# Second feed-forward of a hybrid decoder block: tile pairs three and four moved into the seven-product form

## The chip, the core and the metric

One core of a Trainium2 chip runs the whole block in one program. The metric is the device time of that program in microseconds (us): 994.03 us is the median of three runs before the change. The engines named below are TensorE (PE, its matmuls; PEld, its weight loads), VectorE (DVE), ScalarE (ACT), GpSimd (POOL) and the queue that issues the loads (SP).

## The reference, cut to what matters

The block is a feed-forward, a token mixer, a second feed-forward and a final norm, for one sequence of 512 tokens and D_MODEL = 1024, all in float32. The change is in the second feed-forward; D_FF is 2816, which makes 22 tiles of 128 in each half of `w_in`.

```
def swiglu(u, w_in, w_out):
    a, b = jnp.split(u @ w_in, 2, axis=-1)
    return (jax.nn.silu(a) * b) @ w_out
...
        u = modulate(rmsnorm(h, g_norm_ffn2[l]), sh3, sc3)
        h = h + 0.5 * gt3 * swiglu(u, w_ffn2_in[l], w_ffn2_out[l])
    return rmsnorm(h, g_final)
```

## The kernel before, in words

**Number format.** Every float32 operand x is held as two tiles, a rounded high part (ACT copies it, L319 for weights) and a low part x - high (DVE subtracts, L333 for weights). A product is three matmuls: high by high, high by low, low by high (`mm3`, L364 to L366). The activations u of the norm stand in UH and UL: 8 slices (k) of 512 tokens, whose halves the code calls A (tokens 0 to 255) and Bh.

**Weights.** SP loads 128x1024 pieces into three `raw` buffers (and, in the feed-forwards, into parts of the tile X that have come free). `split_hi` makes the high part in a ring `whi`, `split_lo` the low part in a ring `wlo`; the rings hold seven such pieces and 128 columns over. A piece that would run over the ring's end is written in two parts, 896 and 128 columns. `take` hands out the next piece; `look(n)` splits up to n pieces ahead. For some pieces (`self.outer`) the low part is not made by DVE: ACT writes minus the high part to `wlo` (L315) and a POOL DMA adds the weight to it (L317).

**Plain pairs.** Tile pair j is the 128 columns j of the a half and of the b half. In the plain form a pair takes 48 matmuls with 512 tokens each (`ffn_tile`, twice).

**Seven products.** `duo(j)` does pairs j and j+1 together: the 2x2 block product in seven block products instead of eight, with sums of blocks on both sides. Product i is `product(...)`, 24 matmuls of 256 tokens (L755 to L757). The seven pieces of weights, in order, are r11, x0 = r12 - r11, x1 = r22 - x0, r21, r12 (replaced by r22 - r12), r22, x0 = r21 - x1; DVE makes the differences (`make`, L258). On the side of u, the blocks of sums S0, S1, S2 (`SH`/`SL`) and S3 (put over the first half of u in the second token half) come from `u_steps` once per feed-forward: sums on DVE (L714), high parts on ACT (L719), low parts on DVE (L722). The products use u itself, S0, S1, u, S2, S3, u. Product 0 goes to PSUM bank A, which ACT copies to bank C before product 2 adds to A (`copy(C, A)`, L762); after product 4 ACT copies A to a tile `u3`, before product 6 adds to A.

**Order of work.** Nothing is reordered by a scheduler: each engine runs its instructions in the order in which the code issues them, and waits in place. Before the change the second feed-forward (n = 2) runs like this: `head` computes pairs 0 and 1 in two token halves (four tiles of weights taken at once, 96 matmuls for each half) while the norm is still producing u (L472 scales to `ut`, L484 writes UH, L489 a plain copy of u for the sums, L498 UL), with three splits in between (`split(self.done)`); in the middle PE needs the row statistics of the second half (ACT square root L457, DVE reciprocal L460, PE spread L465). `ffn2` then runs seven of `u_steps`, `ffn_post` for pairs 0 and 1 (silu on ACT L685, product on DVE L658, split L667/L668), the plain pairs 2 and 3, `duo(4)`, and goes on with `out_quad` (the output matrix, in the same seven-product form) and further `duo`s.

Of the kernel before, what the change touches and what calls it, by code (L numbers as in the profile page):

```python
# [124 lines left out]

PLAIN = {0: 8, 2: 4}
PARTS = ((0, 4), (4, 8), (8, 12), (12, 16), (16, 20), (20, 22))
# [15 lines left out]
class Kernel:  # L143
# [6 lines left out]
    def plan(self):  # L150
# [21 lines left out]
        def blocks(recs, outer=0, rest=()):  # L172
            n = len(self.loads)
            if outer:
                self.outer.update({len(self.order) + 3: n + 3, len(self.order) + 5: n + 2})
            if outer == 3:
                self.outer[len(self.order)] = n
# [18 lines left out]
        def ffn(n, ins, outs, first):  # L196
# [4 lines left out]
            for part, (k0, k1) in enumerate(PARTS):  # L201
                while j < pairs_before(n, part):
                    if j < PLAIN[n]:
                        plain(ins[at:at + 2])
                        if n and j < 2:
                            shift(2)
                        j, at = j + 1, at + 2
                    else:
                        blocks(ins[at:at + 4], 2 if j > PLAIN[n] else 0)
                        j, at = j + 2, at + 4  # L210
# [270 lines left out]
    def norm_u(self, n, k, hs, t, rest=True):  # L481
# [3 lines left out]
        if n == 0 and rest:  # L485
            self.norm_x(k, hs, t)
        if n == 2 and (hs.start or k < 4):
            u = self.U4[1][k // 4] if hs.start else self.cs
            act(u[:, k % 4 * HT:(k % 4 + 1) * HT], t[:, hs], AF.Identity, bias=S, scale=1.0)  # L489
# [34 lines left out]
    def out_tail(self, ms, ksrc, gate, nxt, squares):  # L524
# [7 lines left out]
        for h, hs in enumerate((A, Bh)):  # L532
            for m in ms:
# [20 lines left out]
                if h == 1:  # L554
                    self.held = starts[m + 1]
                    if step:
                        step(1 if m != ms[-1] else 3)
                self.split_lo()
# [58 lines left out]
    def head(self, n, banks, table):  # L617
# [7 lines left out]
        both, late = list(range(4)), (0, 1, 2)  # L625
        steps = [(k, late) for k in range(4)] + [(k, (3,)) for k in range(4)] + [(k, both) for k in range(4, KT)]
        for h, hs in enumerate((A, Bh)):
            for i, (k, which) in enumerate(steps if h == 0 else [(k, both) for k in range(KT)]):
# [11 lines left out]
                if h == 0 and i < 4:  # L640
                    for x, y in ((0, 0), (1, 0), (0, 1)):
                        for j in which:
                            self.nc.tensor.matmul(banks[j][:, hs], w[j][k][x], (self.UH, self.UL)[y][k][:, hs],
                                                  start=k == x == y == 0, stop=False)
                    continue
                for j in which:
                    self.mm3(banks[j][:, hs], *w[j][k], self.UH[k][:, hs], self.UL[k][:, hs], k == 0, k == KT - 1)
                if (h, i) in ((0, 8), (1, 2), (1, 5)):
# [59 lines left out]
    def u_steps(self, n):  # L708
# [17 lines left out]

        def whole(u, k):
            x = slice(k, k + 4)
            hi, lo = (y.rearrange("p (k t) -> p k t", k=KT)[:, x, :HT] for y in (self.UHv, self.ULv))
            return lambda: v.tensor_tensor(u.rearrange("p (k t) -> p k t", k=4), hi, lo, op=OP.add)  # L730

        return ([whole(a12, 4)] if n else []) + [
            add(a22, a21, a22, OP.add), both(high(0, a22), add(a21, a11, a21, OP.subtract)),
            both(high(2, a21), low(0, a22)), add(a11, a22, a11, OP.subtract), both(high(1, a11), low(2, a21)),
            add(a12, a12, a11, OP.subtract), low(1, a11)], both(high(3, a12), low(3, a12))

# [22 lines left out]
    def duo(self, j, first):  # L759
# [64 lines left out]
    def h_sums(self, k0, first):  # L824
# [17 lines left out]
        for n, what in enumerate(((lambda: add(h22, h21, h22, OP.add),),  # L842
# [4 lines left out]
            for f in what:  # L847
                self.later((2 if k0 + 4 > first else 4) + n, f)

# [202 lines left out]
    def ffn2(self):  # L1052
# [24 lines left out]
    def open_ffn(self, nh):  # L1077
# [8 lines left out]
        self.Xall = xp.tile([P, 4 * D], F32, name="X")  # L1086
        a11, a21, a12, a22 = (self.Xall[:, i * D:(i + 1) * D] for i in range(4))
        if nh == 6:
            self.kept, a11 = [self.cond, self.AR, a11], self.cs
        self.U4, self.X, self.rawx = ((a11, a12), (a21, a22)), [a11, a21], [a12, a22]  # L1090
        return st
# [13 lines left out]
    def ffn(self, n, j, last=None):  # L1105
# [12 lines left out]
        for part, (k0, k1) in enumerate(PARTS[:-1]):  # L1118
            while j < pairs_before(n, part):
# [3 lines left out]
                else:  # L1123
                    if j == k1:
                        self.h_sums(k0, PLAIN[n])
                    self.duo(j, last)
# [702 lines left out]
```

## Time and profile before

| what | value |
|---|---|
| median of three runs | 994.03 us (993.3 to 995.08) |
| the profiled execution: its own time | 995.64 us |
| its span, first to last instruction | 993.8 us |
| granted TensorE clock, mean | 0.994 |
| second feed-forward: first matmul of `head` | 655.89 us |
| ... first plain pair after `head` | 680.06 us |
| ... first matmul of the first `duo` | 701.85 us |

Rows of the timeline read: start, duration, engine, line, operation, output<-inputs, shape, count, and in brackets how long the engine stood idle before and what ended that. Where two instructions of an engine follow each other without idle time, the difference of their starts is what the first costs. Rows of the windows give, for a stretch, the busy time of each engine, then the granted clock and the share of the DMA engines.

### The profile page before, as it was taken

The page shows a single profiled execution, that of the slowest core. Times are in us where ns is not written, and L with a number is a line of the kernel's source. Part 1 is how long each engine was busy: PE and PEld are TensorE (multiplying, and loading weights), DVE is VectorE, ACT ScalarE, POOL GpSimd, SP SyncE. Part 2 cuts the span into 40 slices and gives each one's busy share as a digit, 9 for nine tenths or more (in the row PEclk, how much of TensorE's full clock was granted, in tenths as well). Part 3 has the DMA queues.
Part 4 walks back from the last instruction along what each step waited for, and adds up shares of the span by engine and source line. Part 5 has one row for each costly group of instructions (what it writes and reads, how often), then busy time and mean ns, then how long its engine had stood idle before and what let it go on. Part 6 is the DMA issues. An engine that isn't in the chain of part 4 may idle for free.

```text
span 993.8 us, 17278 instructions
## 1 busy us (share of the span) xinstructions
PE 981.3 (99%) x6962; PEld 916.8 (92%) x6962; DVE 825.9 (83%) x1258; ACT 567.2 (57%) x869; POOL 72.4 (7%) x82
## 2 busy tenths in 40 slices
PE   8999999999999999999999999999999999999997
PEld 6888899999999999889978888898999999999996
DVE  6979989999998777879567777578898989989875
ACT  6453276786778753233414323455676768677665
POOL 0000010110111000007100000000010010011001
PEclk9999999999999999999999999999999999999998
DMA  9867577877858723123365774333376566667622
GB/s 337 281 206 261 181 185 206 222 185 215 241 145 191 212 70 93 55 94 112 105 231 170 276 247 136 102 88 104 112 181 178 148 170 161 179 141 199 168 46 85
DMA packets 50034, 166.97 MB, mean 168 GB/s; under 512 B 5665, under 2 KB 8993, under 8 KB 49954
## 3 DMA queue, kind: packets, MB, share of 16 engines
q1 hardware_dynamic: 41778, 137.95, 40.5%
q0 software_dynamic: 7488, 27.27, 16.4%
q8 instruction: 54, 0.88, 0.4%
q10 hardware_dynamic: 688, 0.66, 0.2%
q14 instruction: 26, 0.21, 0.1%
HBM read 163.08 MB, written 2.77 MB: 167 GB/s over the span
## 4 chain that ended last, share of the span: by engine, by line
PE 92%; DVE 6%; issue 1%; ACT 1%; DMA 1%; SPq 0%; DVEq 0%; ACTq 0%
PE bank L364 10%; PE bank L756 10%; PE bank L366 10%; PE bank L365 10%; PE bank L755 10%; PE bank L757 10%; PE bank L877 6%; PE bank L876 6%; PE bank L878 6%; PE bank L1759 1%; PE bank L1763 1%; PE bank L1761 1%; PE bank L1350 1%; DVE wlo L333 1%; DVE qz L1275 1%
## 5 line engine op out<-in xcount | busy, mean ns | idle before, releaser
L333 DVE TENSOR_TENSOR wlo<-raw,whi 128x1024 fp32r<-128x1024 f32 (+6 forms) x124 | 135.6, 1103 | 44.5 <-ACT whi L319 44.3
L319 ACT ACTIVATE whi<-raw 128x1024 fp32r<-128x1024 f32 (+5 forms) x157 | 149.3, 963 | 10.7 <-DMA raw<-wf1o 4.9
L364 PE MATMUL bank<-UH,whi 128*128 128x512 f32 (+1 forms) x408 | 151.6, 372 | 0.0
L366 PE MATMUL bank<-UH,wlo 128*128 128x512 f32 (+1 forms) x408 | 147.5, 362 | 0.0
L365 PE MATMUL bank<-UL,whi 128*128 128x512 f32 (+1 forms) x408 | 147.3, 361 | 0.0
L755 PE MATMUL bank<-UH,whi 128*128 128x256 f32 x512 | 141.4, 276 | 0.0
L757 PE MATMUL bank<-UH,wlo 128*128 128x256 f32 x512 | 141.4, 276 | 0.0
L756 PE MATMUL bank<-UL,whi 128*128 128x256 f32 x512 | 141.4, 276 | 0.0
L755 PE MATMUL bank<-SH,whi 128*128 128x256 f32 x384 | 107.0, 279 | 0.0
L757 PE MATMUL bank<-SH,wlo 128*128 128x256 f32 x384 | 106.9, 278 | 0.0
L756 PE MATMUL bank<-SL,whi 128*128 128x256 f32 x384 | 106.8, 278 | 0.0
L319 ACT ACTIVATE whi<-X 128x1024 fp32r<-128x1024 f32 (+2 forms) x98 | 92.0, 953 | 14.8 <-DVE X L258 14.7
L756 PEld LDWEIGHTS bank<-UL,whi 128*128 128x128 f32 x512 | 96.2, 188 | 0.1
L755 PEld LDWEIGHTS bank<-UH,whi 128*128 128x128 f32 x512 | 96.1, 188 | 0.1
L757 PEld LDWEIGHTS bank<-UH,wlo 128*128 128x128 f32 x512 | 96.1, 188 | 0.0
L333 DVE TENSOR_TENSOR wlo<-X,whi 128x1024 fp32r<-128x1024 f32 (+2 forms) x79 | 82.3, 1057 | 12.5 <-ACT whi L319 12.4
L366 PEld LDWEIGHTS bank<-UH,wlo 128*128 128x128 f32 x408 | 76.8, 188 | 12.1
L365 PEld LDWEIGHTS bank<-UL,whi 128*128 128x128 f32 x408 | 76.7, 188 | 11.4 <-issue 0.5
L364 PEld LDWEIGHTS bank<-UH,whi 128*128 128x128 f32 x408 | 76.7, 188 | 11.3 <-issue 0.5
L876 PE MATMUL bank<-HI,whi 128*128 128x256 f32 x288 | 79.9, 277 | 0.0
L877 PE MATMUL bank<-HK,whi 128*128 128x256 f32 x288 | 79.5, 276 | 0.0
L878 PE MATMUL bank<-HI,wlo 128*128 128x256 f32 x288 | 79.5, 276 | 0.0
(355 smaller groups left out, 2481.6 us busy)
## 6 DMA issues: line engine op xcount, KB each, us to landing
ada<-wada SPq DMA_DIRECT2D x47, 512.0 KB, 5.4
raw<-wmix SPq DMA_DIRECT2D x44, 512.0 KB, 4.1
raw<-wf1i SPq DMA_DIRECT2D x33, 512.0 KB, 6.3
raw<-wf2i SPq DMA_DIRECT2D x31, 512.0 KB, 4.6
AR<-wada SPq DMA_DIRECT2D x16, 512.0 KB, 3.7
wlo<-wf2i POOLq DMA_DIRECT2D x16, 512.0 KB, 5.9
raw<-wf1o SPq DMA_DIRECT2D x15, 512.0 KB, 5.2
X<-wf2i SPq DMA_DIRECT2D x13, 512.0 KB, 7.3
```

What stands on the lines that cost most here:

```text
L319: self.nc.scalar.activation(self.hi[:, y], r[:, x], AF.Copy)
L333: self.nc.vector.tensor_tensor(self.lo[:, y], r[:, x], self.hi[:, y], op=OP.subtract)
L364: M(ps, hi, uh, start=start, stop=False)
L365: M(ps, hi, ul, start=False, stop=False)
L366: M(ps, lo, uh, start=False, stop=stop)
L755: M(o, hi, uh, start=start and p == 0 and k == 0, stop=False, skip_group_check=True)
L756: M(o, hi, ul, start=False, stop=False, skip_group_check=True)
L757: M(o, lo, uh, start=False, stop=k == 3, skip_group_check=True)
L876: M(o, hi, uh, start=start and m % 2 == 0 and k == 0, stop=False, skip_group_check=True)
L877: M(o, hi, ul, start=False, stop=False, skip_group_check=True)
L878: M(o, lo, uh, start=False, stop=k == 1, skip_group_check=True)
L1275: self.nc.vector.tensor_scalar(qz[:, (2 * i + h) * P:(2 * i + h + 1) * P], q[:, toks], self.hmask[:, h:h + 1], None, op0=OP.mult)
```

## The change

`PLAIN[2]` goes from 4 to 2: pairs 2 and 3 of the second feed-forward become a `duo(2)` ahead of `duo(4)`, straight behind `head`. What that needs is moved with it:

- the two plain pieces that `head` split ahead, and the next one, are now r11, x0 and x1 of `duo(2)`; r11's low part goes by ACT and POOL DMA (`outer` = 1), and in `duo(4)` two low parts do (`outer` = 2; it had none);
- `norm_u` also writes the plain copy of u for k = 4 to 7 of half A (four more ACT instructions), and the DVE sum that made it from UH and UL (`whole`) goes;
- the sums of u are done in another order: S0, S1, S2, then the sum for S3, with five steps between `head` and `ffn_post`; they stand in other parts of X and in `cs`, the weight differences in `cond` and X, the results `kept` in X, `AR` and `cs`;
- `head` does one norm step fewer in the tail of the mixer before the last sum of squares, and a bank's halves start as one group;
- `duo(2)` looks three to five pieces ahead, not five; PSUM banks are dealt out in another order.

```
-PLAIN = {0: 8, 2: 4}
+PLAIN = {0: 8, 2: 2}
...
-            if outer:
+            if outer > 1:
                 self.outer.update({len(self.order) + 3: n + 3, len(self.order) + 5: n + 2})
-            if outer == 3:
+            if outer in (1, 3):
                 self.outer[len(self.order)] = n
...
-                        blocks(ins[at:at + 4], 2 if j > PLAIN[n] else 0)
+                        blocks(ins[at:at + 4], 2 if j > PLAIN[n] else n // 2)
...
-        if n == 2 and (hs.start or k < 4):
-            u = self.U4[1][k // 4] if hs.start else self.cs
+        if n == 2:
+            u = self.cs if k < 4 and not hs.start else self.U4[1 if hs.start else 0][k // 4]
...
-                        step(1 if m != ms[-1] else 3)
+                        step(1 if m != ms[-1] else 3 if nxt == 1 else 2)
...
-        return ([whole(a12, 4)] if n else []) + [
-            add(a22, a21, a22, OP.add), both(high(0, a22), add(a21, a11, a21, OP.subtract)),
-            both(high(2, a21), low(0, a22)), add(a11, a22, a11, OP.subtract), both(high(1, a11), low(2, a21)),
-            add(a12, a12, a11, OP.subtract), low(1, a11)], both(high(3, a12), low(3, a12))
+        last = both(high(3, a12), low(3, a12))
+        if n:
+            return [add(a22, a21, a22, OP.add), both(high(0, a22), add(a21, a11, a21, OP.subtract)), low(0, a22),
+                    add(a11, a22, a11, OP.subtract), high(1, a11), low(1, a11), high(2, a21), low(2, a21),
+                    add(a12, a12, a11, OP.subtract)], last
...
-            self.look(5)
+            self.look(3 + i // 3 if first and self.nh == 6 else 5)
...
-        self.banks, self.bi = [*f, *bk[:2], f[0], *bk[2:], f[1], *f[2:], *bk[:2], *f[:2]], 0
+        self.banks, self.bi = [*f[:2], bk[0], *f[2:], bk[1], *bk[2:], bk[0], f[2], *f[:2]], 0
...
-        do(3)
+        do(5)
         for j in range(2):
             self.ffn_post(j, self.ffn_silu(j, bk[2 * j]), bk[2 * j + 1], lambda low: (do(1), low()))
-        pa = self.ffn_tile()
         do(len(self.todo))
         self.free.append(self.rawx[1])
-        due = []
-        self.ffn_post(2, self.ffn_silu(2, pa), self.ffn_tile(), due.append)
-        pa = self.ffn_tile(4)
-        due.pop()()
-        self.ffn_post(3, self.ffn_silu(3, pa), self.ffn_tile(5), lambda low: self.later(1, low))
-        self.ffn(2, 4, last)
+        self.ffn(2, 2, last)
...
+            self.U4, self.X, self.rawx = ((self.cs, a12), (a21, a22)), [self.cond, a11], [a12, a21]
+            self.kept = [a22, self.AR, self.cs]
```

How instructions move is shown at three places. The line numbers of the change's file are a few higher (L720 for L714, L725 for L719, L728 for L722, L664 for L658, L673/L674 for L667/L668, L691 for L685, L767 for L762).

In the order rows a number behind a name tells buffers of one name apart. Rows of the two kernels stand apart.

**First place: DVE at the end of `head`'s second token half.** Before, from the low part for k = 5 to the first sums of u (`ut` is the scaled norm, `UL` its low part, `wlo` the low part of a piece of weights, `cs` and X hold blocks of u):

```order
L498 SCALAR_TENSOR_TENSOR UL<-ut,mod,UH 128x256
L333 TENSOR_TENSOR wlo<-raw_67,whi 128x1024
L472 SCALAR_TENSOR_TENSOR ut<-H_79,mod,bank_97 128x256
L498 SCALAR_TENSOR_TENSOR UL<-ut,mod,UH 128x256 x2
L730 TENSOR_TENSOR X<-UH,UL 128x1024
L714 TENSOR_TENSOR X<-X 128x1024
L714 TENSOR_TENSOR X<-cs,X 128x1024
```

The same place in the changed kernel:

```order
L498 SCALAR_TENSOR_TENSOR UL<-ut,mod,UH 128x256
L258 TENSOR_TENSOR X<-raw_68,cond 128x1024
L333 TENSOR_TENSOR wlo<-cond,whi 128x1024
L472 SCALAR_TENSOR_TENSOR ut<-H_79,mod,bank_97 128x256
L498 SCALAR_TENSOR_TENSOR UL<-ut,mod,UH 128x256 x2
L333 TENSOR_TENSOR wlo<-X,whi 128x1024
L720 TENSOR_TENSOR X<-X 128x1024
L720 TENSOR_TENSOR X<-cs,X 128x1024
```

The low part ahead of the last scaling is now that of x0 (which stands in `cond`), the weight difference x1 and the low part of x1 stand ahead of the first sum of u, and `whole` (L730) is gone.

**Second place: DVE behind the first two sums of u.** Before, from the product for pair 0 on (`sl` and `u` are silu results, `HI`/`HK` the split results of a pair):

```order
L658 TENSOR_TENSOR cond<-sl,bank_102 128x512
L722 TENSOR_TENSOR SL_6044<-X,SH_6043 128x1024
L668 TENSOR_TENSOR HK<-cond,HI 128x256
L658 TENSOR_TENSOR cond<-u_6322,bank_100 128x512
L714 TENSOR_TENSOR cs<-X,cs 128x1024
L668 TENSOR_TENSOR HK<-cond,HI 128x256
L333 TENSOR_TENSOR wlo<-raw_68,whi 128x1024
```

The same place in the changed kernel, down to the low part of the fourth piece of weights, r21:

```order
L728 TENSOR_TENSOR SL_6040<-X,SH_6039 128x1024
L720 TENSOR_TENSOR cs<-X,cs 128x1024
L664 TENSOR_TENSOR X<-sl,bank_102 128x512
L728 TENSOR_TENSOR SL_6043<-cs,SH_6042 128x1024
L674 TENSOR_TENSOR HK<-X,HI 128x256
L664 TENSOR_TENSOR X<-u_6331,bank_100 128x512
L674 TENSOR_TENSOR HK<-X,HI 128x256
L728 TENSOR_TENSOR SL_6045<-X,SH_6044 128x1024
L720 TENSOR_TENSOR X<-X,cs 128x1024
L258 TENSOR_TENSOR raw_67<-raw_68,raw_67 128x1024
L333 TENSOR_TENSOR wlo<-raw_66,whi 128x896
L333 TENSOR_TENSOR wlo<-raw_66,whi 128x128
```

A low part of S0 and the third sum now stand ahead of the product for pair 0, and r12' = r22 - r12 ahead of the low part of r21, which is now the piece in two parts.

**Third place: ACT from the end of `head` to the first copy of bank A.** Before, the rows behind `head`, then, behind the plain pairs, the rows in the first `duo` up to its copy (L762):

```order
L719 ACTIVATE SH_6043<-X 128x1024
L685 ACTIVATE sl<-bank_98 128x512
L667 ACTIVATE HI<-cond 128x256
L719 ACTIVATE SH_6048<-X 128x1024
L685 ACTIVATE u_6322<-bank_103 128x512
L667 ACTIVATE HI<-cond 128x256
L319 ACTIVATE whi<-raw_68 128x1024
...
L667 ACTIVATE HI<-AR 128x512
L319 ACTIVATE whi<-raw_66 128x1024
L762 ACTIVATE bank_99<-bank_98 128x512
```

In the changed kernel the first `duo` follows `head` at once (the first row is the high part of x1):

```order
L319 ACTIVATE whi<-X 128x1024
L725 ACTIVATE SH_6039<-X 128x1024
L725 ACTIVATE SH_6042<-cs 128x1024
L691 ACTIVATE sl<-bank_98 128x512
L673 ACTIVATE HI<-X 128x256
L691 ACTIVATE u_6331<-bank_103 128x512
L673 ACTIVATE HI<-X 128x256
L725 ACTIVATE SH_6044<-X 128x1024
L319 ACTIVATE whi<-raw_66 128x896
L319 ACTIVATE whi<-raw_66 128x128
L767 ACTIVATE bank_98<-bank_99 128x512
```

All three high parts of sums, both pairs' silu and split, and the two parts of r21's high part now stand between `head` and the copy of bank A.

More of the change, by code (lines that the diff above doesn't have):

```diff
@@ L626, in head, with put @@
         steps = [(k, late) for k in range(4)] + [(k, (3,)) for k in range(4)] + [(k, both) for k in range(4, KT)]
+        M = self.nc.tensor.matmul
+        def put(j, k, x, y):
+            M(banks[j][:, hs], w[j][k][x], (self.UH, self.UL)[y][k][:, hs], start=h == k == x == y == 0,
+              stop=k == KT - 1 and x == 1, skip_group_check=True)
         for h, hs in enumerate((A, Bh)):
@@ L642, in head @@
                         for j in which:
-                            self.nc.tensor.matmul(banks[j][:, hs], w[j][k][x], (self.UH, self.UL)[y][k][:, hs],
-                                                  start=k == x == y == 0, stop=False)
+                            put(j, k, x, y)
                     continue
                 for j in which:
-                    self.mm3(banks[j][:, hs], *w[j][k], self.UH[k][:, hs], self.UL[k][:, hs], k == 0, k == KT - 1)
+                    for x, y in ((0, 0), (0, 1), (1, 0)):
+                        put(j, k, x, y)
                 if (h, i) in ((0, 8), (1, 2), (1, 5)):
@@ L725, in both @@
             return lambda: [f() for f in fs]
[L727 to L730, printed above, removed]
-        return ([whole(a12, 4)] if n else []) + [
-            add(a22, a21, a22, OP.add), both(high(0, a22), add(a21, a11, a21, OP.subtract)),
-            both(high(2, a21), low(0, a22)), add(a11, a22, a11, OP.subtract), both(high(1, a11), low(2, a21)),
-            add(a12, a12, a11, OP.subtract), low(1, a11)], both(high(3, a12), low(3, a12))
+        last = both(high(3, a12), low(3, a12))
[3 more added lines that the diff above has]
+                    add(a12, a12, a11, OP.subtract)], last
+        return [add(a22, a21, a22, OP.add), both(high(0, a22), add(a21, a11, a21, OP.subtract)),
+                both(high(2, a21), low(0, a22)), add(a11, a22, a11, OP.subtract), both(high(1, a11), low(2, a21)),
+                add(a12, a12, a11, OP.subtract), low(1, a11)], last
     def step(self):
@@ L847, in h_sums @@
             for f in what:
-                self.later((2 if k0 + 4 > first else 4) + n, f)
+                self.later((2 if k0 > first else 4) + n, f)
     def out_quad(self, k0, gate, tail=None):
@@ L1087, in open_ffn @@
         a11, a21, a12, a22 = (self.Xall[:, i * D:(i + 1) * D] for i in range(4))
+        self.U4, self.X, self.rawx = ((a11, a12), (a21, a22)), [a11, a21], [a12, a22]
         if nh == 6:
-            self.kept, a11 = [self.cond, self.AR, a11], self.cs
-        self.U4, self.X, self.rawx = ((a11, a12), (a21, a22)), [a11, a21], [a12, a22]
+            self.U4, self.X, self.rawx = ((self.cs, a12), (a21, a22)), [self.cond, a11], [a12, a21]
+            self.kept = [a22, self.AR, self.cs]
         return st
@@ L1124, in ffn @@
                     if j == k1:
-                        self.h_sums(k0, PLAIN[n])
+                        self.h_sums(k0, 0 if n else 4)
                     self.duo(j, last)
```

## The prediction

> **What bounds the kernel now.** First the page: how busy each engine is, and of what the chain that ended last consists.
>
> ```profile
> PE 981.3 (99%) x6962; PEld 916.8 (92%) x6962; DVE 825.9 (83%) x1258; ACT 567.2 (57%) x869; POOL 72.4 (7%) x82
> ...
> PE 92%; DVE 6%; issue 1%; ACT 1%; DMA 1%; SPq 0%; DVEq 0%; ACTq 0%
> ```
>
> PE bounds the program. Any edit counts by the matmul time that it removes and the waits that it brings to PE. Next the windows of the stretches that change: the plain pairs, the first `duo`, a later `duo` (us of window; PE, PEld, DVE, ACT, POOL busy; clock).
>
> ```profile
> 680.06:701.85 21.79, 21.79 (x99) 18.02 (x98) 20.43 (x22) 11.79 (x16) 0.00 (x0) 1.00 0.30 97
> 701.85:721.17 19.32, 19.32 (x169) 19.32 (x168) 16.78 (x20) 14.10 (x19) 0.93 (x1) 1.00 0.50 144
> 740.21:759.41 19.20, 19.20 (x170) 19.20 (x169) 16.34 (x22) 9.82 (x14) 1.29 (x2) 1.00 0.64 168
> ```
>
> PE is full in all three, at clock 1.00. But behind `head` DVE is nearly full too (20.43 of 21.79): the plain pairs are when DVE catches up on the sums of u. The timeline of PE gives the borders and the only wait of this feed-forward before its last stage, 0.48 for the norm.
>
> ```profile
> 662.55 0.71 PE L465 MATMUL bank<-cst,r 128*128 128x128 f32 x4 [0.48 <-DVE r L460]
> ...
> 680.06 0.39 PE L364 MATMUL bank<-UH,whi 128*128 128x512 f32 x1
> ...
> 701.85 0.28 PE L755 MATMUL bank<-UH,whi 128*128 128x256 f32 x1
> 704.67 0.28 PE L755 MATMUL bank<-SH,whi 128*128 128x256 f32 x1
> 707.55 0.28 PE L755 MATMUL bank<-SH,whi 128*128 128x256 f32 x1
> 710.29 0.28 PE L755 MATMUL bank<-UH,whi 128*128 128x256 f32 x1
> ```
>
> Products 0, 1 and 2 of the first `duo` take 2.82, 2.88 and 2.74; the rest, (721.17 - 710.29) / 4 = 2.72 each.
>
> **Matmuls, -2.59.** Gone: 21.79 + 19.32 = 41.11. In their place a first `duo` at 19.32 and a steady one at 19.20, 38.52. Eight products of work become seven, but 96 matmuls of 512 take 21.79 and 168 of 256 take 19.3, so the step is worth 12%, and 2.59 us. That the first `duo` keeps its pace beside `head`'s debris is the assumption; pitches of 2.72 against 2.88 bound it at 10 x 0.14 = 1.4 either way, and I take 0.
>
> The Trainium skill ("TensorE: Matmul & The Clock Gate", section "Back-to-back issue gap") states a sustained 131 ns per matmul of 512 and 81 ns per one of 128. By it the plain pairs would take 96 x 0.131 = 12.6 us, and 168 matmuls of a width between would take 13.6 us or more, so this change would lose time on PE itself. The trace's 21.79 / 96 = 227 ns speaks against it, and the sum doesn't use it.
>
> **Four more ACT copies in half A, +0.17.** ACT at the end of half A with DVE's reciprocal, and what a copy costs (starts 0.40 apart):
>
> ```profile
> 655.69 0.50 ACT L489 ACTIVATE cs<-ut,mod 128x256 f32<-128x256 f32 x1
> 656.09 0.49 ACT L484 ACTIVATE UH<-ut,mod 128x256 fp32r<-128x256 f32 x1
> ...
> 659.82 0.51 ACT L484 ACTIVATE UH<-ut,mod 128x256 fp32r<-128x256 f32 x1 [0.52 <-DVE ut L472]
> 660.61 0.51 ACT L484 ACTIVATE UH<-ut,mod 128x256 fp32r<-128x256 f32 x1 [0.28 <-DVE ut L472]
> 661.39 0.51 ACT L484 ACTIVATE UH<-ut,mod 128x256 fp32r<-128x256 f32 x1 [0.28 <-DVE ut L472]
> 661.81 0.24 ACT L457 ACTIVATE r<-bank,eps 128x2 f32<-128x2 f32 x1
> 662.34 0.16 DVE L460 RECIPROCAL r<-r 128x2 f32<-128x2 f32 x1
> ...
> 663.81 0.51 ACT L484 ACTIVATE UH<-ut,mod 128x256 fp32r<-128x256 f32 x1 [0.46 <-DVE ut L472]
> ```
>
> Most of four copies (1.6) fits into waits of 0.52, 0.28 and 0.28. The square root moves from 661.81 to 662.23 and ends at 662.47; the reciprocal, which stood at 662.34 behind DVE's last UL, goes to 662.51. PE's spread moves from 662.55 to 662.72, and so does all behind it. If the copies hid wholly it is 0, with none hidden 1.6; I take 0.17.
>
> **Three splits in half B, and when u's sums can start.** In half B ACT now has work where it waited (1.68 at 668.16 before):
>
> ```profile
> 668.16 0.51 ACT L484 ACTIVATE UH<-ut,mod 128x256 fp32r<-128x256 f32 x1 [1.68 <-DVE ut L472]
> ```
>
> UH of k = 0 starts at 663.98 (663.81 + 0.17). Four activations at 0.40 bring ACT to 665.60, minus r11 and r11's high part (0.97 each, from 678.23 to 679.20 in the rows below) to 667.54, ten activations to 671.54; x0's high part ends at 672.58 (1.04, from 708.25 to 709.29 below). Then DVE, which ran here before:
>
> ```profile
> 674.39 0.47 DVE L472 SCALAR_TENSOR_TENSOR ut<-H,mod,bank 128x256 f32<-128x256 f32 x1
> ...
> 675.84 1.22 DVE L730 TENSOR_TENSOR X<-UH,UL 128x1024 f32<-128x1024 f32 x1
> 676.97 1.22 DVE L714 TENSOR_TENSOR X<-X 128x1024 f32<-128x1024 f32 x1
> 678.23 1.22 DVE L714 TENSOR_TENSOR X<-cs,X 128x1024 f32<-128x1024 f32 x1
> 679.83 0.69 DVE L658 TENSOR_TENSOR cond<-sl,bank 128x512 f32<-128x512 f32 x1 [0.38 <-ACT sl L685]
> 680.43 1.22 DVE L722 TENSOR_TENSOR SL<-X,SH 128x1024 fp32r<-128x1024 f32 x1
> 681.57 0.42 DVE L668 TENSOR_TENSOR HK<-cond,HI 128x256 fp32r<-128x256 f32 x1
> ```
>
> A DVE piece costs 1.13 (675.84 to 676.97), or 1.26 where it waits for the one ahead (676.97 to 678.23). x0's low part runs 672.62 to 673.75, the last scaling 0.47; ACT's UH, copy and x1's high part end at 676.10 (674.26 + 2 x 0.40 + 1.04); x1's low part ends at 677.27. **The first sum starts at 677.27, against 676.97**, although `whole` is gone.
>
> **The wait at product 2, +3.62.** It adds to bank A, so it must wait for ACT's copy to C, and that copy stands behind all of the `head` work. ACT's prices:
>
> ```profile
> 678.23 1.06 ACT L719 ACTIVATE SH<-X 128x1024 fp32r<-128x1024 f32 x1 [2.42 <-DVE X L714]
> 679.20 0.60 ACT L685 ACTIVATE sl<-bank 128x512 f32<-128x512 f32 x1
> ...
> 704.93 0.58 ACT L762 ACTIVATE bank<-bank 128x512 f32<-128x512 f32 x1 [0.58 <-PE bank L757]
> ...
> 708.25 1.14 ACT L319 ACTIVATE whi<-cs 128x896 fp32r<-128x896 f32 x2
> 709.29 1.05 ACT L319 ACTIVATE whi<-raw 128x1024 fp32r<-128x1024 f32 x1
> ```
>
> By DVE's new order: sums at 677.27 and 678.53 (+1.26), low S0 at 679.66, the third sum at 680.79, there at 682.01. ACT: high S1 at 682.05, silu of pair 0 at 683.02 (+0.97), done 683.62. DVE: its product at 683.66, low S1 at 684.26 (+0.60), the split's low half at 685.39 (+1.13), pair 1's product at 685.79 (0.42 long, 0.40 of pitch), there at 686.48 (0.69). ACT: pair 1's high half at 686.52, high S2 at 686.92, r21's high part in two pieces at 687.89 (+0.97), the copy at 688.93 (708.25 to 709.29 is 1.04), done at 689.51; product 2 starts at 689.55. It is due at 680.06 + 0.17 + 2.82 + 2.88 = 685.93: **PE waits 3.62**. In the old place the copy waited for PE (0.58 at 704.93), not the other way round. Bounds: 0 if the copy is ready; 5.1 if the 1.4 above falls on the chain.
>
> **Second wait, product 6, +0.67.** Behind that, DVE runs without a pause. High S2 ends at 687.98, so low S2 runs to 689.15 and the sum for S3 to 690.28; r12' to 691.41, low r21 in two parts to 692.62 (product 3, due at 692.29, starts with its first part), low S3 to 693.75, then low r12', x0', low r22 and low x0' (4 x 1.13) to 698.27. There stands the next `duo`'s x0, to 699.49. ACT's high part of that (0.97) is ahead of its copy to `u3`, which so starts at 700.50 and ends at 701.08. Product 6 is due at 689.55 + 2.74 + 3 x 2.72 = 700.45 and starts at 701.12. Third, in `duo(4)`: DVE, still without a pause, has r12' at 705.74, behind it stand about 3.4 of ACT work (three pieces of weights, a silu) and the copy to C, done at 709.76; product 2 is due at 701.12 + 2 x 2.72 + 2.86 = 709.42: **+0.38**. For each of the two, 0 to 1.4 as above.
>
> **r21's low parts on the POOL queue, 0.** An issue by POOL and how long such a transfer takes to land:
>
> ```profile
> 756.13 0.87 POOL L317 DMA_DIRECT2D wlo<-wf2i  x1 [15.50 <-ACT wlo L315]
> ...
> wlo<-wf2i POOLq DMA_DIRECT2D x3, 512.0 KB, 5.5
> ```
>
> Later blocks issue that piece in two DMAs. POOL had been idle 15.50, so a second issue (0.87) is no queue; it lands at about 756.13 + 2 x 0.87 + 5.5 = 763.4, and its product starts at 759.41 + 3 x 2.75 = 767.7. What hides it is 4 us of lead; without it each block would lose up to 0.9.
>
> **Sum:** -2.59 + 0.17 + 3.62 + 0.67 + 0.38 = +2.25, and about 0.35 for three more hand-offs at 1.26 instead of 1.13 in the chain: **+2.6**. The profiled execution has a span of 993.8 and its own time is 995.64, 1.6 above the median of 994.03; the sum is a difference of spans, so it is put on the median: **996.6**.
>
> **The rivals.**
>
> *A, faster: the copy is hidden, as in the old place.* Only -2.59 + 0.17 remain: 991.6. It decides itself at one point: the copy must start by 685.93 - 0.62 = 685.31, so the first sum by about 673.65. DVE is busy 20.43 of 21.79 behind `head`, which speaks against.
>
> *B, the clock halves after the first long wait.* Here is the one place ahead of the last stage where the granted clock fell:
>
> ```profile
> 13.00:14.00 1.00, 0.83 (x5) 0.57 (x6) 1.00 (x6) 0.26 (x1) 0.00 (x0) 0.67 1.10 422
> 14.00:15.00 1.00, 1.00 (x5) 1.00 (x6) 0.81 (x6) 0.94 (x2) 0.00 (x0) 0.50 1.02 404
> 15.00:16.00 1.00, 1.00 (x7) 1.00 (x6) 0.10 (x1) 0.32 (x1) 0.00 (x0) 0.50 1.04 414
> 16.00:17.00 1.00, 1.00 (x8) 1.00 (x7) 1.00 (x2) 0.32 (x1) 0.00 (x0) 0.62 1.00 397
> ```
>
> Lost work there: 0.33 + 0.50 + 0.50 + 0.38 = 1.71 us. Of that the later waits take back 0.67 to 1.05, so this gives 997.3 to 998.3. For it: the clock fell there though PE was busy 0.83 or more of each window. Against: no wait of such a length stands in this trace.
>
> The Trainium skill says on the same page, section "Why this matters for your kernels", that gaps of over about 3 us between matmuls bring the half clock back. The trace has no such gap to agree or differ.
>
> *C, the second load into X is late.* It is issued after low S3, at 693.8, and needed at 698.3, 4.5 later; loads of this kind took 3.9 into `raw` but 7.0 into X:
>
> ```profile
> raw<-wf2i SPq DMA_DIRECT2D x13, 512.0 KB, 3.9
> X<-wf2i SPq DMA_DIRECT2D x4, 512.0 KB, 7.0
> ```
>
> At 7.0, product 6 is 2.5 later: 999.1.
>
> *D, a part of the wait.* If the chain is shorter by about half (DVE and ACT slots that I put in series overlap), 994.0 to 995.8: no change that can be told.
>
> **How the numbers follow.** Forecast 0.52 (996.6, between 995.8 and 997.6), A 0.11, B 0.22, C 0.05, D 0.10. A measurement of this kernel tells about 0.2%, or 2.0 us, from no change: below 992.0 is faster, above 996.0 slower. A is faster but for 0.02; D and a small part of the forecast (0.08) lie within: faster 0.09, same 0.20, slower 0.71. The range leaves out A, half of D and C: 995.0 to 999.0.
>
> **What would show it.** A PE wait of 3 to 4 us, at the first matmul of product 2 of the first `duo` (near 686), ended by ACT's copy of bank A; a smaller one at product 6, ended by the copy to `u3`; the first sum of u near 677.3; clock 1.00 behind the wait (else B); the two stretches at 19.3 and 19.2 without their waits. No wait at product 2 makes the prediction wrong, and so does any wait over 0.5 in the later `duo`s, which the sum puts at nothing.

## The result, and the profile after

The changed kernel takes **998.68 us** (median of 6 runs, 998.4 to 1000.51) against 994.31 of the kernel before (6 runs, 993.3 to 995.54): ratio 1.0046, 95% interval 1.0033 to 1.0059, so 4.4 us slower. The forecast was 996.6, slower, with a range of 995.0 to 999.0.

Executions differ by up to 3 us in when `head` starts (655.27 here, 658.43 in that of e1_fill further down). So the two profiled executions (spans of 996.8 and 993.8) are compared from `head`'s first matmul to the first matmul of the `duo` behind the first `out_quad`. First the windows of the kernel before: that whole stretch, and the `out_quad` in it.

```profile
655.89:740.21 84.32, 83.84 (x634) 79.87 (x633) 75.40 (x104) 58.88 (x92) 3.10 (x4) 1.00 0.41 115
721.17:740.21 19.04, 19.04 (x170) 19.04 (x169) 19.02 (x25) 16.43 (x23) 2.17 (x3) 1.00 0.69 169
```

The changed kernel: the whole, then `head`, `duo(2)`, `duo(4)` and the `out_quad`.

```profile
655.27:743.73 88.46, 83.76 (x707) 83.35 (x705) 80.02 (x105) 68.09 (x109) 8.24 (x10) 0.96 0.51 128
655.27:679.01 23.74, 23.07 (x203) 22.86 (x201) 20.16 (x39) 19.20 (x39) 0.94 (x1) 1.00 0.26 65
679.01:705.37 26.36, 22.33 (x170) 22.13 (x169) 23.66 (x25) 16.70 (x25) 1.76 (x2) 0.87 0.43 122
705.37:724.69 19.32, 19.32 (x171) 19.32 (x169) 17.77 (x19) 15.77 (x22) 2.63 (x3) 1.00 0.72 175
724.69:743.73 19.04, 19.04 (x171) 19.04 (x169) 18.42 (x24) 16.42 (x24) 2.91 (x4) 1.00 0.69 165
```

The stretch grew by 88.46 - 84.32 = 4.14, which is the measured 4.4 within its interval. `duo(4)` and the `out_quad` keep 19.32 and 19.04. All of the loss is in `duo(2)`: 26.36 where the plain pairs took 21.79; PE works 22.33 of it, at a mean clock of 0.87. PE's rows there show both halves of it: starts of products 0, 1, 2, 3 and 4.

```profile
679.01 0.28 PE L760 MATMUL bank<-UH,whi 128*128 128x256 f32 x1
681.73 0.28 PE L760 MATMUL bank<-SH,whi 128*128 128x256 f32 x1
688.77 0.58 PE L760 MATMUL bank<-SH,whi 128*128 128x256 f32 x1 [4.03 <-ACT bank L767]
694.06 0.29 PE L760 MATMUL bank<-UH,whi 128*128 128x256 f32 x1
696.89 0.28 PE L760 MATMUL bank<-SH,whi 128*128 128x256 f32 x1
```

Product 2 waits 4.03 for ACT's copy of bank A (L767), and then takes 5.29 (688.77 to 694.06), where the same product took 2.74 before. The windows of those microseconds say why; the column behind POOL's is the granted clock:

```profile
686.00:687.00 1.00, 0.00 (x0) 0.00 (x0) 0.43 (x1) 1.00 (x2) 0.00 (x0) 1.00 0.00 0
687.00:688.00 1.00, 0.00 (x0) 0.00 (x0) 0.76 (x1) 1.00 (x3) 0.00 (x0) 0.61 0.00 0
688.00:689.00 1.00, 0.23 (x1) 0.23 (x2) 1.00 (x2) 0.72 (x3) 0.00 (x0) 0.50 0.00 0
693.00:694.00 1.00, 1.00 (x6) 1.00 (x6) 1.00 (x2) 0.25 (x1) 0.00 (x0) 0.50 0.00 0
694.00:695.00 1.00, 1.00 (x10) 1.00 (x9) 1.00 (x2) 0.60 (x1) 0.00 (x0) 0.98 0.96 180
```

A mean of 0.61 is 0.78 us of that window at half. So the clock halves at 687.2, inside the wait, and comes back at 694.0, 6.8 us later. Until then the matmuls of product 2 start 0.21 us apart, and not 0.11 to 0.12.

### The profile page after: what moved, and what is told of

Read it like the earlier page. It is cut to its first block, busy times and chain, and to the rows that moved or that the text cites. A ratio compares the mean times of both kernels' runs of the same rounds, so it can differ in the third digit from the quotient of the medians.

```text
span 996.8 us, 17470 instructions
## 1 busy us (share of the span) xinstructions
PE 980.1 (98%) x7034; PEld 919.5 (92%) x7034; DVE 830.0 (83%) x1247; ACT 578.0 (58%) x896; POOL 87.9 (9%) x99
## 4 chain that ended last, share of the span: by engine, by line
PE 91%; DVE 6%; ACT 1%; issue 1%; DMA 1%; DVEq 0%; ACTq 0%
PE bank L760 11%; PE bank L762 11%; PE bank L761 11%; PE bank L364 8%; PE bank L366 8%; PE bank L365 8%; PE bank L881 6%; PE bank L882 6%; PE bank L883 6%; PE bank L630 3%; PE bank L1759 1%; PE bank L1761 1%; PE bank L1763 1%; PE bank L1350 1%; DVE wlo L333 1%
## 5 line engine op out<-in xcount | busy, mean ns | idle before, releaser
L762 PE MATMUL bank<-UH,wlo 128*128 128x256 f32 x544 | 150.3, 276 | 0.0
L762 PE MATMUL bank<-SH,wlo 128*128 128x256 f32 x408 | 114.6, 281 | 0.0
L364 PE MATMUL bank<-UH,whi 128*128 128x512 f32 x272 | 109.8, 404 | 0.0
L366 PE MATMUL bank<-UH,wlo 128*128 128x512 f32 x272 | 106.0, 390 | 0.0
L365 PE MATMUL bank<-UL,whi 128*128 128x512 f32 x272 | 106.0, 390 | 0.0
L319 ACT ACTIVATE whi<-X 128x1024 fp32r<-128x1024 f32 (+4 forms) x107 | 95.6, 912 | 17.7 <-DVE X L258 17.4
L760 PEld LDWEIGHTS bank<-UH,whi 128*128 128x128 f32 x544 | 102.4, 188 | 0.0
L761 PEld LDWEIGHTS bank<-UL,whi 128*128 128x128 f32 x544 | 102.2, 188 | 0.0
L762 PEld LDWEIGHTS bank<-UH,wlo 128*128 128x128 f32 x544 | 102.1, 188 | 0.0
L760 PEld LDWEIGHTS bank<-SH,whi 128*128 128x128 f32 x408 | 78.1, 192 | 4.2 <-ACT bank L767 4.2
L761 PEld LDWEIGHTS bank<-SL,whi 128*128 128x128 f32 x408 | 78.2, 192 | 0.0
L762 PEld LDWEIGHTS bank<-SH,wlo 128*128 128x128 f32 x408 | 78.1, 191 | 0.0
```

The costliest lines, as they stand in the source:

```text
L319: self.nc.scalar.activation(self.hi[:, y], r[:, x], AF.Copy)
L364: M(ps, hi, uh, start=start, stop=False)
L365: M(ps, hi, ul, start=False, stop=False)
L366: M(ps, lo, uh, start=False, stop=stop)
L760: M(o, hi, uh, start=start and p == 0 and k == 0, stop=False, skip_group_check=True)
L761: M(o, hi, ul, start=False, stop=False, skip_group_check=True)
```

## The experiments

Nine kernels went to the chip. Each one's time stands beside runs of the kernel before on the same chip (medians 994.3 to 994.9). "Stretch" is from `head`'s first matmul to the third `duo`, in the profiled execution, against 84.32 before.

| kernel | median us | ratio to before, 95% interval | stretch | longest wait of PE in it |
|---|---|---|---|---|
| changed | 998.68 | 1.0046 (1.0033 to 1.0059) | 88.46 | 4.03 |
| e1_fill | 997.13 | 1.0021 (1.0009 to 1.0032) | 86.90 | 0.57 |
| e2_fill12 | 997.82 | 1.0029 (1.0016 to 1.0042) | 86.88 | 2.61 |
| e3_copy_early | 998.58 | 1.0044 (1.0028 to 1.0059) | 88.11 | 3.20 |
| e4_reordered | 994.95 | 1.0008 (0.9996 to 1.0020) | 84.73 | 0.84 |
| e5_old_sums | 997.18 | 1.0028 (1.0015 to 1.0040) | 86.49 | 3.08 |
| e6_reordered2 | 995.60 | 1.0000 (0.9987 to 1.0013) | 84.09 | 0.53 |
| e7_r11_low_by_dve | 999.82 | 1.0043 (1.0026 to 1.0060) | 88.90 | 4.87 |
| e8_reordered3 | 993.44 | 0.9985 (0.9974 to 0.9997) | 83.34 | 0.80 |
| e9_reordered3b | 993.32 | 0.9984 (0.9973 to 0.9996) | 82.40 | 0.67 |

### e1_fill and e2_fill12: is the slow product 2 the clock?

```
+            if i == 2 and first and self.nh == 6:
+                for k in range(30):            # e2_fill12: 12
+                    matmul(self.banks[self.bi][:, :HT], self.UH[0][:, :P], self.UH[k % 4][:, T1], start=True, stop=True)
             self.product(bank, u, start)
```

> Changed kernel (998.68) with 30 matmuls of 256 (about 3.4 us) into an unused PSUM bank between products 1 and 2 of the first duo: PE works through most of the 4.03 us for which it waited; what ends the wait stays. If the slow product 2 (5.29 instead of 2.74) is the clock, dropped by the gap: the clock stays at 1.00 from 684 to 700, product 2 takes 2.75 to 2.85, and product 6 and duo(4)'s product 2 now wait, 0.4 to 0.7 each, as the prediction had it without rival B; so 997.0 to 997.6. If the fillers keep nothing (the clock falls for another reason, or product 2 is slow for its operands): 998.5 to 998.9.

> As e1_fill with 12 matmuls (1.4 us): a gap of about 2.65 us is left instead of 4.03. If a gap must last over 3 us or so to drop the clock: clock 1.00 and the time of e1_fill, 997.0 to 997.6. If any stretch in which PE is idle more than half the time drops it: half clock near 687.4 to 694 as in the changed kernel, and 998.5 to 998.9.

Both first cases came in the traces; of the times, e1_fill's lies in its range and e2_fill12's median of 997.82 lies 0.2 above it. PE's remaining waits in e1_fill, and a window of the product behind the first:

```profile
691.95 0.39 PE L760 MATMUL bank<-SH,whi 128*128 128x256 f32 x1 [0.46 <-ACT bank L767]
703.76 0.39 PE L760 MATMUL bank<-UH,whi 128*128 128x256 f32 x1 [0.57 <-ACT u L767]
...
692.00:694.00 2.00, 2.00 (x17) 2.00 (x18) 2.00 (x3) 1.13 (x2) 0.00 (x0) 1.00 0.48 158
```

The copy still ends the wait: product 2 starts 4.2 after product 1 has ended, but the clock stays at 1.00 and it takes 2.85. And the wait at product 6, which the forecast had at 0.67, is there: 0.57, where the changed kernel had none. The forecast's third wait came back too: products 1 and 2 of `duo(4)` take 5.90 (709.51 to 715.41) and not the 5.61 of the changed kernel. So the half clock cost 2.55, but about 1.0 of that would have gone into later waits anyway, 0.57 and 0.29 of it into these two: 998.68 - 997.13 = 1.55 net, and 88.46 - 86.90 = 1.56 in the stretch. With 12 fillers the gap is 2.61, the clock held in this execution, and the two later waits are there again:

```profile
688.51 0.38 PE L760 MATMUL bank<-SH,whi 128*128 128x256 f32 x1 [2.61 <-ACT bank L767]
700.31 0.39 PE L760 MATMUL bank<-UH,whi 128*128 128x256 f32 x1 [0.29 <-ACT u L767]
709.13 0.38 PE L760 MATMUL bank<-SH,whi 128*128 128x256 f32 x1 [0.23 <-ACT bank L767]
...
687.00:688.00 1.00, 0.00 (x0) 0.00 (x0) 1.00 (x1) 1.00 (x3) 0.00 (x0) 1.00 0.00 0
688.00:689.00 1.00, 0.49 (x4) 0.49 (x5) 1.00 (x2) 0.45 (x1) 0.00 (x0) 1.00 0.00 0
```

It seems not to hold in each: 2 of the 11 runs have a mean clock of 0.993 (the changed kernel's runs have 0.993 to 0.995, e1_fill's 0.996 to 0.998) and 998.1 to 998.2 us, near the changed kernel's time. Of these two no trace was kept, so that the clock fell behind this gap is read from their means alone. By them, a gap of 2.6 is about where it may fall or not.

### e3_copy_early: is it only the place of the copy?

```
-        do(5)
+        do(4)
+        self.first_product()      # product 0, then copy(C, A)
+        do(1)
...
-            self.look(3 + i // 3 if first and self.nh == 6 else 5)
+            self.look((2 if i == 0 else 3 + i // 3) if pre else 5)
...
 the banks, in words:
-  [f0, f1, bk0, f2, f3, bk1, ..., bk0, f2, f0, f1]
+  [f0, f1, f2, bk0, f3, bk1, ..., f2, bk0, f0, f1]
```

> Changed kernel with ACT's copy of bank A to C issued before the high part of S1 (product 0 is issued before that in the program; banks f[2] and bk[0] change names so that the copy overwrites nothing that is still read). Theory (the backlog of sums, splits and pair results on DVE and ACT is the cause, the copy only stands last in it): product 2 then waits about 1.1 for S1's low part and product 3 about 3.5 to 4 for r21's high and low part; waits of 5 us in place of 4.0, and 998.5 to 1001. Rival (the place of the copy in ACT's queue is the cause): the wait goes to under 1 and the clock stays, 992 to 994.

In this kernel and in e4_reordered, bank C is another one than in the changed kernel, and the outcome is not complete. Most likely product 3 does not add to the copy that ACT put into bank C, so that one block product of pairs 2 and 3 is missing; no run was made to show that. No instruction is fewer (7034 matmuls in the changed kernel and in both), so the times can be compared. The theory's case came, with 4.5 of wait instead of the 5 that it gave. PE's waits in `duo(2)`:

```profile
685.96 0.39 PE L761 MATMUL bank<-SL,whi 128*128 128x256 f32 x1 [1.00 <-DVE SL L728]
689.13 0.38 PE L760 MATMUL bank<-UH,whi 128*128 128x256 f32 x1 [0.27 <-ACT whi L319]
692.83 0.39 PE L762 MATMUL bank<-UH,wlo 128*128 128x256 f32 x1 [3.20 <-DVE wlo L333]
```

The copy no longer holds anything up; now DVE's low part of S1 does for 1.00, ACT's high part of r21 for 0.27 and DVE's low part of r21 for 3.20: 4.47 in all instead of 4.03. The wait is the backlog on DVE and ACT, and the copy stood last in it. Here, too, the clock fell, later and for half as long:

```profile
694.00:695.00 1.00, 1.00 (x9) 1.00 (x8) 1.00 (x2) 0.79 (x2) 0.00 (x0) 0.64 0.00 0
695.00:696.00 1.00, 1.00 (x6) 1.00 (x6) 1.00 (x2) 0.00 (x0) 0.00 (x0) 0.50 0.93 168
696.00:697.00 1.00, 1.00 (x7) 1.00 (x6) 1.00 (x2) 0.58 (x1) 0.00 (x0) 0.50 0.87 320
697.00:698.00 1.00, 1.00 (x8) 1.00 (x8) 1.00 (x2) 1.00 (x2) 0.00 (x0) 0.65 0.92 295
```

That is (0.36 + 0.50 + 0.50 + 0.35) / 0.5 = 3.4 us at half clock, from 694.3 on, though PE has worked again since 692.83.

### e5_old_sums: the new order of the sums undone

```
-            return [S0, high 0 + S2, low 0, S1, high 1, low 1, high 2, low 2, S3]
+            return [S0, high 0 + S2, high 2 + low 0, S1, high 1 + low 2, S3, low 1]
```

> Changed kernel with the sums of u in the order of before (S2's high part with S0's low, S1's high with S2's low, S3's sum, S1's low last, seven steps instead of nine), all else as changed. By the prices of the rows S1's sum is a step earlier, pair 0's product does not stand behind it on DVE, and S2 is done when r21's turn comes, so the copy of bank A comes about 0.9 earlier. Theory (the backlog and its order make the wait): the wait at product 2 falls from 4.03 to about 3.1. If the clock still falls in that gap: 997.5 to 998; if it holds (it held in a gap of 2.6 and fell in one of 3.2): 995 to 995.6. Rival (the new order of the sums is what makes the wait short, as the diff would have it): a longer wait than 4.03 and over 999.

```profile
687.83 0.58 PE L760 MATMUL bank<-SH,whi 128*128 128x256 f32 x1 [3.08 <-ACT bank L767]
...
687.20 0.58 ACT L767 ACTIVATE bank<-bank 128x512 f32<-128x512 f32 x1
```

The wait is 3.08 and the copy starts 0.95 earlier than the 688.15 of the changed kernel: the part of the change that reorders the sums makes the wait longer, against the rival. The time, 997.18, is 0.3 below the first of the two cases: the clock did fall, but for (0.30 + 0.50 + 0.50 + 0.41) / 0.5 = 3.4 us and not 6.8, and product 2 took 4.26 instead of 5.29.

```profile
687.00:688.00 1.00, 0.17 (x1) 0.17 (x2) 1.00 (x2) 1.00 (x4) 0.00 (x0) 0.70 0.00 0
688.00:689.00 1.00, 1.00 (x5) 1.00 (x6) 1.00 (x2) 1.00 (x2) 0.00 (x0) 0.50 0.08 16
689.00:690.00 1.00, 1.00 (x7) 1.00 (x6) 1.00 (x3) 1.00 (x2) 0.00 (x0) 0.50 0.00 0
690.00:691.00 1.00, 1.00 (x7) 1.00 (x7) 1.00 (x2) 1.00 (x2) 0.00 (x0) 0.59 0.00 0
```

### e7_r11_low_by_dve: the POOL way for r11's low part undone

```
-                        blocks(ins[at:at + 4], 2 if j > PLAIN[n] else n // 2)
+                        blocks(ins[at:at + 4], 2 if j > PLAIN[n] else 0)
```

> Changed kernel without the POOL way for the first weight piece of duo(2) and for duo(4): DVE makes r11's low part in head's second half (1.13 more of DVE) and ACT writes no minus r11 (0.97 less of ACT). Theory (head's second half is bound by DVE behind ACT's splits, and every 1 us there shifts the first sum of u and so the copy): the first sum starts 0.7 to 0.9 later, the wait at product 2 grows from 4.03 to about 4.8, 999.2 to 999.8. Rival (there is slack in front of the first sum, the wait is made behind it): wait and time as changed, 998.5 to 998.9.

The edit takes the POOL way from `duo(2)` alone: `duo(4)` still issues its three POOL transfers (two at 705.49, one at 710.13), though the expectation names it as well. The first sum of u is at 678.50, 15.40 behind PE's spread (663.10), against 676.67 and 14.55 in the changed kernel: 0.85 later. The wait grows by 0.84:

```profile
690.60 0.58 PE L760 MATMUL bank<-SH,whi 128*128 128x256 f32 x1 [4.87 <-ACT bank L767]
```

As the theory had it, there is no slack ahead of the first sum, and this part of the change takes 0.8 off the wait. The stretch is only 0.44 longer than the changed kernel's (88.90 against 88.46): behind the half clock products 4 to 6, and product 0 of `duo(4)`, took 2.72 each here and 2.83 there. By the ratios to the kernel before (1.0043 and 1.0046) the two times are not told apart. The clock was at half from 689.3 to 696.1, 6.8 us; the first and the last window of that:

```profile
689.00:690.00 1.00, 0.00 (x0) 0.00 (x0) 0.94 (x1) 1.00 (x4) 0.00 (x0) 0.65 0.00 0
...
696.00:697.00 1.00, 1.00 (x10) 1.00 (x10) 1.00 (x2) 0.60 (x1) 0.00 (x0) 0.94 0.70 164
```

### e4_reordered and e6_reordered2: the backlog moved into idle time

```
 sums and splits behind head, in order of issue (e6_reordered2):
+  S0, high 0, S2, product 0, high r21, low 0, S1, low r21, high 1, low 1, silu 0, copy(C, A),
+  product of pair 0, r12', high 2, low half of pair 0, silu 1, product of pair 1, low 2, ..., S3
-            self.look(3 + i // 3 if first and self.nh == 6 else 5)
+            self.look((2, 3, 3, 3, 2, 3, 4)[i] if pre else (3, 4, 4, 4, 4, 5, 5)[i] if j == 4 and self.nh == 6 else 5)
             elif i == 2:
                 copy(c0, r(A))
+                if pre:
+                    first()               # S3, which was behind product 0
```

> Changed kernel with the backlog put into the idle time of ACT and DVE: r21 is split between the sums of u (ACT waited 2.4 there), S1 ahead of the pairs' results, the copy behind S1's high part, r12' ahead of S3, S3 behind the copy of product 2, and duo(2) and duo(4) split 2 to 4 pieces ahead instead of 3 to 5. Theory (the step is worth 2.6 of matmuls and everything lost is wait and clock): no wait over 1, waits of about 1.5 in all in products 6, and of duo(4); clock 1.00; 993.2 to 994.2, so 4.5 to 5.5 under the changed kernel and at or a little under the kernel before. Rival (the seven products cost more here than 38.5, or DVE's total is the bound whatever the order): over 995.

> As e4_reordered with the copy of bank A behind pair 0's silu instead of ahead of it, so that bank C stays the one of the changed kernel and product 3 adds to the copy; r12' ahead of S2's high part; duo(4) splits one piece less ahead at its fifth product. Nothing of the computation is left out. Waits of about 1.1 in all, the longest 0.3 to 0.4, clock 1.00. Theory (the step is worth 2.0 to 2.6 of matmuls, all of its loss is wait and clock): 1.0 to 1.8 under the kernel before, 992.7 to 993.5. Rival (the seven products cost more here than they save): at or over the kernel before, 994.3 or more.

Not in the cut: DVE makes the weight differences of `duo(2)` no longer a piece ahead until its product 3 (`eager`). The long wait and the half clock are gone (the clock is 1.00 over the whole stretch in both), so the wait and the clock did carry the loss of the changed kernel. But neither kernel beats the one before: ratios 1.0008 and 1.0000, and for e6_reordered2 the time of the rival came. What is left there, beyond a wait of 0.15 and the one of 0.39 below, shows in the windows of `duo(4)` and of the `out_quad`:

```profile
716.64 0.39 PE L762 MATMUL bank<-UH,wlo 128*128 128x256 f32 x1 [0.39 <-DMA wlo<-wf2i]
...
701.99:722.17 20.18, 19.79 (x171) 19.60 (x170) 19.46 (x20) 17.17 (x25) 4.31 (x5) 1.00 0.73 185
722.17:742.10 19.93, 19.93 (x170) 19.85 (x169) 19.93 (x26) 16.68 (x25) 2.72 (x4) 1.00 0.72 172
```

The same 168 matmuls of the `out_quad` that took 19.04 take 19.93, with PE busy throughout at full clock: 0.119 per matmul instead of 0.113. The wait of 0.39 stands 5.5 ahead of it, in `duo(4)`. It is a wait for the POOL transfer of r22's low part (product 5), for which the changed kernel did not have to wait: it comes to that product 64.0 us behind `head`'s first matmul, e6 after 57.9. e4_reordered has the same wait, 0.34.

### e8_reordered3 and e9_reordered3b: the last waits moved

```
+  e8: product 0, S0, high 0, S2, high r21, S1, low r21, low 0, high 1, low 1, silu 0, copy(C, A),
+      product of pair 0, silu 1, r12', high 2, ...
+  e9: product 0, S0, high 0, S2, high r21, low 0, S1, low r21, high 1, ...
+  both: look (3, 3, 3, 4, 2, 3, 3) in duo(2); in duo(4) r21's low part by DVE, not by POOL
```

> As e6_reordered2, with the steps behind head in yet another order (product 0 and r21's high part first, S1's sum and r21's low part ahead of S0's low part, both silus ahead of S2), other look-ahead numbers, and in duo(4) r21's low part made by DVE instead of a POOL transfer. The order leaves one wait of about 0.8, at product 1 (S0's low part), and no other over 0.1 up to the second out_quad. e6 showed waits of 0.15 and 0.39 behind which PE ran at 0.118 us per matmul instead of 0.1133 for whole products. Theory (with the waits gone the step is worth its 2.0 to 2.6; what is lost is each wait and the slower pace behind it): 1.5 to 2.5 under the kernel before, 992.0 to 993.3. Rival (the pace is slow here whatever the waits; the seven products save nothing in this place): within 0.5 of e6, 994.3 or more.

> e8_reordered3 with S0's low part ahead of S1's sum again: the one wait of 0.8 then stands at product 5 (S3's low part) instead of product 1, and the pace behind it has no S0 product to reset it until duo(4). Theory (a wait costs itself and the slower pace up to the next S0 product): the wait 0.8 plus 0.3 to 0.5, so 0.3 to 0.5 more than e8, 992.4 to 993.8. Rival (where a wait stands makes no difference): the time of e8 within 0.1.

In both, the weight differences are made ahead again from product 2 on. These are the versions that beat both kernels, by a little: 993.44 and 993.32, ratios 0.9985 and 0.9984, with intervals that end just below 1 (0.9997 and 0.9996), both against the same runs of the kernel before. The theory's 1.5 to 2.5 is not reached in the medians (0.9 and 1.0). In the profiled execution of e9 the whole stretch is 1.92 shorter than before, in that of e8 0.98. The window of e9, its wait at product 5, and the two waits of e8:

```profile
655.33:737.73 82.40, 81.30 (x706) 80.72 (x705) 78.70 (x105) 65.47 (x106) 6.19 (x7) 1.00 0.46 130
...
693.71 0.39 PE L763 MATMUL bank<-UL,whi 128*128 128x256 f32 x1 [0.43 <-DVE UL L730]
...
682.47 0.39 PE L763 MATMUL bank<-SL,whi 128*128 128x256 f32 x1 [0.80 <-DVE SL L730]
724.04 0.39 PE L895 MATMUL bank<-ut,whi 128*128 128x256 f32 x1 [0.29 <-ACT bank L873]
```

e8's wait of 0.80 came where it was expected; the one of 0.29, in the `out_quad`, was not expected. Behind it PE ran at 0.118, and that `out_quad` took 20.13, against 19.36 in e9: most of the 0.94 between the two stretches. The expectation of e9 had the slow pace in e9, and there it did not come. In the times, where the last wait stands made no difference that could be measured (0.12 between the medians, against intervals of about 1.1 to each side); the wait at product 5 was 0.43 and not 0.8.

## Why the prediction was right or wrong, point by point

The sign, the mechanism and its place were right; the likeliest case had no half clock, and that is the step that failed. That 998.68 lies within 995.0 to 999.0 is owed to the upper end, which was set wide enough for rival B, and in part to luck: three terms of 1.40 in all that did not come, and 0.62 that `head` gained, hid most of the 2.55 that the half clock cost. The terms, in the stretch from `head` to the third `duo`:

| term | forecast | measured | from |
|---|---|---|---|
| matmuls | -2.59 | -2.01 | 26.36 + 19.32 - 4.03 - 2.55 = 39.10, against 41.11 |
| four copies in half A | +0.17 | +0.19 | spread at 662.12 - 655.27 = 6.85, against 6.66 |
| `head` behind the spread | 0 | -0.62 | 679.01 - 662.12 = 16.89, against 17.51 |
| wait at product 2 | +3.62 | +4.03 | PE's row |
| half clock in product 2 | 0 (rival B: 1.71) | +2.55 | 5.29 against 2.74 |
| wait at product 6, at `duo(4)`'s product 2 | +0.67, +0.38 | 0, 0 | no such wait |
| more hand-offs | +0.35 | 0 | below |
| sum | +2.6 | +4.14 | |

**The chain on DVE and ACT held to 0.2.** The rows of the changed kernel: DVE's first and third sum, its product for pair 1, and ACT's last two steps ahead of product 2.

```profile
676.67 1.22 DVE L720 TENSOR_TENSOR X<-X 128x1024 f32<-128x1024 f32 x1
680.23 1.22 DVE L720 TENSOR_TENSOR cs<-X,cs 128x1024 f32<-128x1024 f32 x1
685.13 0.68 DVE L664 TENSOR_TENSOR X<-u,bank 128x512 f32<-128x512 f32 x1
...
687.11 1.13 ACT L319 ACTIVATE whi<-raw 128x896 fp32r<-128x896 f32 x2
688.15 0.57 ACT L767 ACTIVATE bank<-bank 128x512 f32<-128x512 f32 x1
```

The first sum stands 14.55 behind the spread (676.67 - 662.12), and the forecast had 677.27 - 662.72 = 14.55. The copy stands 26.03 behind it, forecast 26.21; so the 0.35 that was added for hand-offs was not needed. e7 confirms the part ahead of the first sum (0.85 for one DVE piece less one ACT piece), e5 the part behind it.

**The wait was 0.4 longer because PE came earlier.** The 144 matmuls of `head` behind the spread ran at 0.114 and not at 0.118, which the prediction had put at no change, so product 2 was due at 684.74, 22.62 behind the spread, against 23.21 forecast: 0.59 more wait from there, 0.18 less from the chain. What `head` gained, the wait took back at once. The gain belongs to the change and not to one execution: in all ten traces of kernels with the change these matmuls ran at 0.114, in the one trace without it at 0.118. The change gives them other start flags (a bank's halves start as one group); whether that is the reason, no run shows.

**The half clock is the step that failed.** It was rival B, with a chance of 0.22, under half of that of a clock that holds, and a price of 1.71 less what later waits take back. Its mechanism was right: the wait at product 6 and the one in `duo(4)` did vanish, and both returned in e1_fill once the clock held. Its size was too small: 1.71 was taken from a stretch of 3.4 us at half clock, and here it was 6.8 us, of which 5.3 fell on PE's work and cost 2.55. (Its upper end, too, was added wrongly: 996.6 + 1.71 - 0.67 is 997.6; 998.3 takes nothing back. So was the upper bound of the wait, 3.62 + 1.4, which is 5.0 and not 5.1.) The gaps of the runs: 4.03 and 4.87 gave 6.8 us at half clock each, 3.08 and 3.20 gave 3.4, 2.61 gave none in the trace and, by the mean clock, in 9 of 11 runs. The Trainium skill ("TensorE: Matmul & The Clock Gate", section "Why this matters for your kernels") warns of idle gaps over about 3 us between matmuls. The runs agree with it: of the gaps above, those from 3.08 on lost the clock; that the one of 2.61 may have lost it in 2 of 11 runs makes it no sharp border.

**The matmul term was 0.6 too large** in its size: products 3 to 6 of `duo(2)` and product 0 of `duo(4)` took 2.83 each, 0.118 per matmul, where 2.72 was taken: five times 0.11. The bound of 1.4 that was given for the pace covers it.

**The rivals.** A (the copy is hidden) was out by 4.0; e3 shows that even a copy in time would only have passed the wait on. C did not come: no wait for a load is in the rows. D did not come. Making the low parts of r21 and r22 by POOL cost nothing in the changed kernel, as taken: `duo(4)` and the `out_quad` are unchanged. That holds only while PE is as late as there: e4_reordered and e6_reordered2 waited 0.34 and 0.39 for such a transfer, and e8 and e9, with one low part fewer on POOL, did not.

**What became of the 2.6 that the step is worth.** In the place that it was put it starts with a DVE that had 20.43 of 21.79 to do behind `head`. The plain pairs used neither the sums of u nor a copy of a bank, so that work could spread over their 21.79 us; the first `duo` needs, within 6 us, the first sums, the split pieces and the copy that stands behind them. e4, e6, e8 and e9 give most of that backlog to idle times of ACT and DVE, and end, by the medians, between 0.7 over and 1.0 under the kernel before. What still keeps them from the 2.6 is in part the slower pace of PE, and its reason stays open.

## What to carry to other kernels

Before a form with fewer matmuls replaces a plain one, count what the other engines must have done by its second or third step, in the order of their queues: here the chain gave 3.6 of wait by plain addition of rows. In this kernel a PE wait of 3 to 5 us cost its length plus 1.5 to 2.6 for the half clock; a run of throwaway matmuls into an unused bank won 1.55 of that back. And a wait's releaser is only the last in a queue: before it is moved, ask what stands next.

## What the runs showed of the hardware

- The clock fell inside the gap (changed kernel: at 687.2, gap ended at 688.77) or up to 1.5 us after its end (e3: gap ended at 692.83, clock at half from 694.3), and then stayed at half for 3.4 us or twice that, although PE was busy again.
- A stream of 256-wide matmuls has two paces at full clock, 0.113 and about 0.118 us, over whole stages: `head` behind the spread ran at 0.118 before and 0.114 after with the same operands in the same order (but other start flags), the `out_quad` of e6 at 0.119. The slow pace often follows a short wait, but not always: the spread's wait of 0.67 was followed by the fast one, and in e2_fill12 the wait of 0.29 ended a slow stretch. What sets it stays open; no run here was made for it alone.
